# Three-part products with the low factors last, and transposes moved behind every second half-unit

## The chip, the cores and the metric

One core of a Trainium2 chip. The metric is the time of one execution on the device in microseconds; a kernel is run three times and the median is taken. One execution more is recorded by the hardware profiler. Its engines are called PE (TensorE), DVE (VectorE), ACT (ScalarE), POOL (GpSimd) and SP (SyncE) here, as in the profile.

## The reference

One inference step of a two-layer encoder for 512 frames of a new stream and 8 × 16 frames of running streams, 640 rows of 1024 values in all, float32. Each layer is a half-step SwiGLU FFN, a mixer, and another half-step FFN; each sub-layer ends in a layer norm:

```python
x = layer_norm(ALPHA * x + 0.5 * swiglu(x, ffn_w_gate[l, 0], ffn_w_up[l, 0], ffn_w_down[l, 0]), ...)
m = mixer_ab(...) if l % 2 == 0 else mixer_ssd(...)
x = layer_norm(ALPHA * x + m, ...)
x = layer_norm(ALPHA * x + 0.5 * swiglu(x, ffn_w_gate[l, 1], ffn_w_up[l, 1], ffn_w_down[l, 1]), ...)
```

The FFN is 1024 to 2816 to 1024. The first mixer is an S5 state-space model beside stick-breaking attention; the second is a Mamba-2 mixer (`mixer_ssd`): one projection to z, x, B, C and dt, a causal convolution of width 4, a chunked recurrence, a gate with an RMS norm, and an output projection. Nearly all of the arithmetic lies in the projections.

## The kernel before

**Three-part products.** Every float32 operand of a projection is held as two tiles of type float32r: a high part, made by a copy on ACT, and a low part, the rest, made by a subtraction on DVE (`split`, L99 to L101; one layer norm further, L210 and L211 do the same for x). A product of two such operands is three matmuls: high × high, low × high, high × low. They are added up in one PSUM bank over all K tiles of 128 rows. Three functions write such products:

- `mm3` (L140): the projections of both mixers, the first units and the down-projections of the FFNs. For each K tile it issues the three parts, then goes on to the next K tile.
- `product` in `ffn` (L362): the gate and up projections of all four FFNs multiply pairs of units by a seven-product scheme. Each of the seven is 4 K tiles × 3 parts with 320 columns.
- `product` in `down7` (L497): the same scheme for most of the down-projection in FFN 1 to 3, 2 K tiles × 3 parts with 512 columns.

The attention part of the first mixer has a list of matmuls of its own (`three`, issued at L1044 in an order that is fixed by hand).

**Stages.** They run in the order FFN 0, mixer 0, FFN 1, FFN 2, mixer 1, FFN 3. Activations `xt` are held channel by channel, once as high and once as low part, 8 K tiles of 640 columns. Channel-wise projections (`cm_proj`) handle them in two halves, `HALVES`: rows 0 to 255 (a matmul of 256 columns) and rows 256 to 639 (384 columns). One half of one unit of 128 output channels is called a half-unit here: 24 matmuls. Row-wise projections (`tm_proj`) add into `yacc`, 5 tiles of 128 rows, called t = 0 to 4.

**Layer norms and transposes.** `layer_norm` (L174) works on one tile t of `yacc`: statistics on DVE (L181, L182), the power on POOL (L184), and then for t < 4 a pass on ACT (L188), DVE (L190) and three on POOL (L191 to L193), for t = 4 two passes on DVE (L195, L197). After that the tile has to be turned for the next stage: eight transposes on PE (L209), whose results ACT (L210, high) and DVE (L211, low) copy out. They are not issued at once but put on a list, `pend`; `run_pend` (L165) issues the oldest entry. A stage ends with `run_pend` at t = 2, 3 and 4, so two entries, t = 3 and t = 4, are left for the stage behind it. There they are issued between the first half-units, which need only t = 0 and 1. Half-units of the second half need t = 2 to 4.

**The start of mixer 1.** `xbc_half(g, u, h)` computes half h of one unit of x, B or C, `gate_half` one of z, `dt_half` one of dt. Today each of the three ends in a `run_pend`. The first calls are

```python
xbc_half(0, 0, 0)
xbc_half(0, 1, 0)
dt_half(0)
gate_half(0, 0, 0)
xbc(0, 0)
```

where `xbc(0, 0)` starts with the second half of unit 0. Later calls find the list empty.

**What sets the order.** The program is written in the order of the source, and the framework gives each engine its instruction list: by priority in source order, with room to put an instruction behind another one whose operands it expects sooner. On the chip each engine then works its list off in order. Weights come by DMA from SP into 4 raw tiles, are converted by ACT and DVE, and wait in 6 pairs of tiles. Matmuls write 8 PSUM banks: kinds a (2), b (4), y and z (1 each).

## Time and profile before

| | |
|---|---|
| three runs | 2533.86, 2541.68, 2542.25 us; median 2541.68 |
| profiled execution | 2534.06 us; span from first to last instruction 2532.4 us |
| DVE busy | 2018.3 us (80% of the span) |
| ACT busy, POOL busy | 1272.1 us (50%), 372.9 us (15%) |
| granted clock of TensorE, mean | 0.997 |
| moved by DMA | 324.80 MB, 128 GB/s |

How to read it: a row of the timeline is "start, duration, engine, line, operation, output <- inputs, shape, count", with the idle time of the engine before it and what ended that in brackets. PE shows matmuls, PEld the loads of their stationary operand. Matmuls are pipelined: a row's duration is the time that one is under way, and the pace is read from start to start. "w" is a converted weight, "xhi" and "xlo" are the parts of x, "h" the FFN's hidden rows, "T" sums of blocks of x, "og" and "csb" the gated rows of mixer 1, "bank" a PSUM bank.

### The profile page before, as it was taken

The page shows a single profiled execution, that of the slowest core. Times are in us where ns is not written, and L with a number is a line of the kernel's source. Part 1 is how long each engine was busy: PE and PEld are TensorE (multiplying, and loading weights), DVE is VectorE, ACT ScalarE, POOL GpSimd, SP SyncE. Part 2 cuts the span into 40 slices and gives each one's busy share as a digit, 9 for nine tenths or more (in the row PEclk, how much of TensorE's full clock was granted, in tenths as well). Part 3 has the DMA queues.
Part 4 walks back from the last instruction along what each step waited for, and adds up shares of the span by engine and source line. Part 5 has one row for each costly group of instructions (what it writes and reads, how often), then busy time and mean ns, then how long its engine had stood idle before and what let it go on. Part 6 is the DMA issues. An engine that isn't in the chain of part 4 may idle for free. (4 is left out here: it accounts for less than half of the span.)

```text
span 2532.4 us, 40815 instructions
## 1 busy us (share of the span) xinstructions
PE 2488.3 (98%) x15551; PEld 2282.8 (90%) x15551; DVE 2018.3 (80%) x3505; ACT 1272.1 (50%) x2389; POOL 372.9 (15%) x492
## 2 busy tenths in 40 slices
PE   9999999999999999999999999999999999999998
PEld 8999999878779999999999999999999879999997
DVE  7788777666878888878988887777576789998887
ACT  4443444336744555553455554566565543554542
POOL 0000001210130000013000002311121151112121
PEclk9999999999999999999999999999999999999999
DMA  5332335443221433462144434456464722555563
GB/s 186 109 101 87 107 118 155 144 160 109 84 84 59 116 104 98 113 162 68 59 113 112 121 100 131 150 163 196 151 214 135 244 72 94 158 149 164 154 173 115
DMA packets 179253, 324.80 MB, mean 128 GB/s; under 512 B 21312, under 2 KB 92608, under 8 KB 178544
## 3 DMA queue, kind: packets, MB, share of 16 engines
q1 hardware_dynamic: 165200, 293.83, 36.7%
q0 software_dynamic: 13856, 28.35, 5.7%
q8 instruction: 122, 2.00, 0.3%
q14 instruction: 75, 0.61, 0.1%
HBM read 259.56 MB, written 40.54 MB: 119 GB/s over the span
## 5 line engine op out<-in xcount | busy, mean ns | idle before, releaser
L101 DVE TENSOR_TENSOR w<-raw,w 128x512 fp32r<-128x512 f32 (+2 forms) x721 | 626.4, 890 | 84.0 <-ACT w L100 81.2
L100 ACT CAST w<-raw 128x512 fp32r<-128x512 f32 (+1 forms) x721 | 531.5, 769 | 317.2 <-DVE raw L349 153.2
L366 PE MATMUL bank<-xhi,w 128*128 128x320 f32 x2432 | 540.4, 310 | 2.9 <-DVE s L408 1.9
L146 PE MATMUL bank<-xhi,w 128*128 128x256 f32 (+2 forms) x2272 | 497.6, 311 | 6.7 <-DVE hf L288 1.7
L366 PE MATMUL bank<-T,w 128*128 128x320 f32 x2736 | 428.4, 309 | 3.6 <-ACT bank L383 1.7
L366 PEld LDWEIGHTS bank<-xhi,w 128*128 128x128 f32 x2432 | 406.8, 188 | 8.7 <-DVE s L408 3.1
L366 PEld LDWEIGHTS bank<-T,w 128*128 128x128 f32 x2736 | 407.0, 188 | 6.6 <-ACT bank L383 3.9
L146 PEld LDWEIGHTS bank<-xhi,w 128*128 128x128 f32 x2272 | 376.9, 187 | 16.3 <-issue 3.9
L366 PE MATMUL bank<-xlo,w 128*128 128x320 f32 x1216 | 375.2, 309 | 0.0
L146 PE MATMUL bank<-xlo,w 128*128 128x256 f32 (+2 forms) x1136 | 350.5, 309 | 2.0 <-DVE xlo L211 1.8
L146 PE MATMUL bank<-w,h 128*128 128x512 f32 x1488 | 346.5, 391 | 0.0
L146 PEld LDWEIGHTS bank<-w,h 128*128 128x128 f32 x1488 | 277.1, 188 | 57.5 <-ACT h L100 1.4
L366 PEld LDWEIGHTS bank<-xlo,w 128*128 128x128 f32 x1216 | 228.2, 188 | 0.0
L146 PEld LDWEIGHTS bank<-xlo,w 128*128 128x128 f32 x1136 | 213.6, 188 | 3.3 <-DVE xlo L211 2.1
L349 DVE TENSOR_TENSOR raw<-raw 128x512 f32<-128x512 f32 x304 | 211.5, 696 | 3.4
L515 POOL DMA_DIRECT2D yacc<-ev x84 | 72.6, 888 | 689.4 <-ACT ev L514 610.8
L502 PE MATMUL bank<-w,h 128*128 128x512 f32 x576 | 134.5, 389 | 0.0
L502 PEld LDWEIGHTS bank<-w,h 128*128 128x128 f32 x576 | 108.1, 188 | 22.4
L379 ACT COPY mx<-bank 128x320 f32<-128x320 f32 x152 | 64.6, 425 | 104.4 <-PE bank L366 104.1
L511 DVE SCALAR_TENSOR_TENSOR yacc<-bank,yacc 128x512 f32<-128x512 f32 x84 | 57.8, 688 | 72.0 <-PE bank L502 71.9
L223 DVE SCALAR_TENSOR_TENSOR yacc<-bank,yacc 128x512 f32<-128x512 f32 x120 | 81.8, 686 | 34.1 <-PE bank L146 33.4
L514 ACT ACTIVATE ev<-bank 128x512 f32<-128x512 f32 x84 | 50.2, 597 | 116.2 <-PE bank L502 112.9
(437 smaller groups left out, 3427.6 us busy)
## 6 DMA issues: line engine op xcount, KB each, us to landing
raw<-in_w_gate_dram SPq DMA_DIRECT2D x88, 512.0 KB, 3.6
raw<-in_w_up_dram SPq DMA_DIRECT2D x88, 512.0 KB, 4.1
raw<-in_w_down_dram SPq DMA_DIRECT2D x88, 512.0 KB, 3.6
raw<-in_m_in_dram SPq DMA_DIRECT2D x52, 512.0 KB, 4.4
yacc<-ev POOLq DMA_DIRECT2D x84, 256.0 KB, 4.7
raw<-in_m_out_dram SPq DMA_DIRECT2D x24, 512.0 KB, 4.5
csb<-cs_d SPq DMA_DIRECT2D x20, 512.0 KB, 5.3
h<-in_ssd_h_dram SPq DMA_DIRECT2D x16, 512.0 KB, 6.1
```

The costliest lines, as they stand in the source:

```text
L100: nc.scalar.copy(hi, src)
L101: return nc.vector.tensor_tensor(lo, src, hi.bitcast(F32), op=ALU.subtract)
L146: state["pe"] = nc.tensor.matmul(ps, a, b, start=(k == 0), stop=(k == n - 1)).ins
L223: state["acc"] = nc.vector.scalar_tensor_tensor(ya, pb, scale, ya, op0=ALU.mult, op1=ALU.add).ins
L349: V.tensor_tensor(o, v, w, op=ALU.subtract)
L366: nc.tensor.matmul(ps, A[p][:, a, k * 128:k * 128 + 128], X[p][b][:, k, :], start=(first and n == 0), stop=(n == 11), skip_group_check=True)
L379: nc.scalar.copy(e[n], ps)
L502: nc.tensor.matmul(ps, a[:, u], b[:, v], start=(first and n == 0), stop=(n == 5), skip_group_check=True)
L511: V.scalar_tensor_tensor(ya, ps, 0.5 / ALPHA, ya, op0=ALU.mult, op1=ALU.add)
L514: nc.scalar.mul(e, ps, 0.5 / ALPHA)
L515: nc.gpsimd.dma_start(yacc[:, t, 512 * j:512 * j + 512], e, accum_op=ALU.add)
```

## The change

In the three functions the loop over parts becomes the outer one: high × high over all K tiles, then the two products with a low factor, each over all K tiles. In `product` of `ffn` the part with the low moving operand comes second and that with the low weights last; in the other two it is the other way about. The same matmuls add into the same banks. In mixer 1 the three helpers lose their `run_pend`, and two calls are put between the first half-units.

```diff
     def mm3(ps, lhs, rhs):
         n = 3 * len(lhs)
         k = 0
-        for (wh, wl), (xh, xl) in zip(lhs, rhs):
-            for a, b in ((wh, xh), (wl, xh), (wh, xl)):
+        for i, j in ((0, 0), (1, 0), (0, 1)):
+            for a, b in [(w[i], x[j]) for w, x in zip(lhs, rhs)]:
...
             def product(ps, A, p, first):
                 n = 0
-                for k in range(4):
-                    for a, b in ((0, 0), (1, 0), (0, 1)):
+                for a, b in ((0, 0), (0, 1), (1, 0)):
+                    for k in range(4):
                         nc.tensor.matmul(ps, A[p][:, a, k * 128:k * 128 + 128], X[p][b][:, k, :],
...
                 def product(ps, tp, p, first):
                     n = 0
-                    for f in fs[::2]:
-                        a, b = left(f, p, tp), right(f, p)
-                        for u, v in ((0, 0), (1, 0), (0, 1)):
+                    for u, v in ((0, 0), (1, 0), (0, 1)):
+                        for f in fs[::2]:
+                            a, b = left(f, p, tp), right(f, p)
...
                     nc.scalar.copy(es_[:, :, 3:19], ps[:, 512 - o:L].rearrange("p (b i) -> p b i", i=16))
-                run_pend()
...
                 V.scalar_tensor_tensor(s, s, 1.0, ps[:, :L], op0=ALU.add, op1=ALU.mult)
-                run_pend()
...
                 V.tensor_scalar(dt[:, o:o + L], ps[:32, :L], hp[:, 0:1], None, op0=ALU.add)
-                run_pend()
...
             xbc_half(0, 0, 0)
             xbc_half(0, 1, 0)
+            run_pend()
             dt_half(0)
             gate_half(0, 0, 0)
+            run_pend()
             xbc(0, 0)
```

## The prediction

> **What bounds the kernel now.** I read the page first: its span, its busy shares, then the waits of TensorE (columns: engine and line that waited, who ended the wait; us in total, times, longest).

> ```profile
> span 2532.4 us, 40815 instructions
> PE 2488.3 (98%) x15551; PEld 2282.8 (90%) x15551; DVE 2018.3 (80%) x3505; ACT 1272.1 (50%) x2389; POOL 372.9 (15%) x492
> ```

> ```profile
> PE bank L209 <- POOL yacc L192: 4.1, 2, 2.1
> ...
> PE bank L146 <- DVE xlo L211: 1.8, 1, 1.8
> ...
> PE bank L146 <- ACT xhi L210: 1.0, 4, 0.2
> ...
> PE bank L146 <- DVE og L101: 0.8, 1, 0.8
> PE bank L366 <- DVE w L101: 0.7, 1, 0.7
> ```

> TensorE has work in flight for 2488.3 of 2532.4 us, so all waits together are worth 44.1 us (1.7%), and the change adds and removes no instruction. It can act in two ways only: by the pace of the matmuls, or by the few waits that a low part or a pending transpose ends. Those are the five rows above. "bank" is the output; the releaser is what the matmul lacked: 4.1 us for a normalized row (half of it at the point the change moves), 1.8 for the low part of x, 0.8 and 0.7 for low parts of og and w.

> **Pace.** The groups of the lines view by shape (count, busy us, mean ns of one), and two places of the timeline (start, duration):

> ```profile
> L366 PE MATMUL bank<-xhi,w 128*128 128x320 f32 x2432 | 540.4, 310 | 2.9 <-DVE s L408 1.9 <-ACT mx L379 0.7 <-DVE hf L418 0.4
> L366 PE MATMUL bank<-T,w 128*128 128x320 f32 x2736 | 428.4, 309 | 3.6 <-ACT bank L383 1.7 <-ACT w L100 1.2 <-DVE w L101 0.7
> L366 PE MATMUL bank<-xlo,w 128*128 128x320 f32 x1216 | 375.2, 309 | 0.0
> ```

> ```profile
> 101.47 0.31 PE L366 MATMUL bank<-xlo,w 128*128 128x320 f32 x1
> 101.61 0.45 PE L366 MATMUL bank<-xhi,w 128*128 128x320 f32 x2
> 101.91 0.31 PE L366 MATMUL bank<-xlo,w 128*128 128x320 f32 x1
> ```

> From one xlo matmul to the next it takes 0.44 us for three, 147 ns each, and they start evenly (101.47, 101.61): the pair that shares its moving operand gains nothing over the pair that changes both. High and low operands take 310 and 309 ns. So the new order costs 0 in pace. Its bounds on both sides: the rows differ by 1 ns of one matmul, and some 13,000 matmuls come from the three edited functions, so ±13 us if that 1 ns were an effect of order. I take 0, since the difference has the size of the rounding.

> **Part 1, the second mixer's start.** Today transposes follow the first and the second half-unit. The change runs them after the second and the fourth.

> ```profile
> 1589.40 0.48 PE L146 MATMUL bank<-xhi,w 128*128 128x256 f32 x2
> ...
> 1592.10 0.28 PE L146 MATMUL bank<-xlo,w 128*128 128x256 f32 x1
> 1592.67 1.73 POOL L192 TENSOR_TENSOR yacc<-yacc,T 128x512 f32<-128x512 f32 x1
> ...
> 1594.45 1.09 PE L209 MATMUL bank<-ident,yacc 128*128 128x128 f32 x8 [2.08 <-POOL yacc L192]
> ...
> 1598.59 1.27 DVE L197 SCALAR_TENSOR_TENSOR yacc<-yacc,rs,T 128x1024 f32<-128x1024 f32 x1
> ...
> 1600.01 1.07 PE L209 MATMUL bank<-ident,yacc 128*128 128x128 f32 x8
> ...
> 1601.07 0.62 DVE L101 TENSOR_TENSOR w<-raw,w 128x512 fp32r<-128x512 f32 x1
> ...
> 1602.83 1.27 DVE L101 TENSOR_TENSOR w<-raw,w 128x512 fp32r<-128x512 f32 x2
> ...
> 1606.36 0.51 PE L146 MATMUL bank<-xhi,w 128*128 128x384 f32 x2
> ```

> ```profile
> 1595.30:1598.70 3.40, 3.40 (x19) 3.40 (x18) 3.40 (x8) 1.20 (x3) 1.75 (x3) 0.52 0.64 217
> ...
> 469.00:472.00 3.00, 2.55 (x15) 2.56 (x16) 0.99 (x2) 0.00 (x0) 0.00 (x0) 1.00 1.00 356
> ...
> 1700.00:1720.00 20.00, 20.00 (x145) 19.07 (x144) 14.58 (x26) 12.33 (x35) 2.96 (x8) 1.00 0.58 166
> ```

> The first half-unit runs from 1589.40 to 1592.2 (24 matmuls, 2.81 us). Then TensorE stands for 2.08 us, since GpSimd ends row t=3 only at 1594.40. In the windows view the next 3.40 us have a granted clock of 0.52 (the column behind POOL): another 3.40 × 0.48 = 1.6 us. So the stall costs 3.7 us. After the 1.81 us stall of the mixer 0 start (second row) the clock is 1.00.

> [...]

> After the change t=3 is due at 1589.40 + 2 × 2.81 = 1595.0, later than 1594.40: no stall. Eight transposes take 0.87 us (1600.01 less its tail), so the third and fourth half-unit end at 1601.5; t=4 (DVE L197, ended 1599.86) is ready by then, the transposes end at 1602.4. What is late next: the unit behind them reads t=4 at once, where today 5.5 us lie between; the four such places in the waits table cost 0.2 us each, and an activation stands ahead of the copies, so 0.5 us. The second-half unit then starts at 1602.9 against 1606.36: 3.5 us gained at most. Against it: the gate unit's weights. I take the conversion at 1601.07 for the second half of its low part and the pair at 1602.83 for the unit behind it. TensorE would reach those low weights after three half-units, eight transposes and 12 more matmuls, 1589.40 + 8.4 + 0.9 + 1.4 = 1600.1, and DVE has them at 1601.69: 1.6 us back, 1.9 gained. DVE runs without a break here (3.40 of 3.40 us in the first windows row), but its order will be dealt anew, and the transposes' low parts leave the way. I take 2.5 (range 1.9 to 3.5; 0.3 if the new stall reaches 2 us and halves the clock again). It stays gained: in the mixer behind it TensorE is the busy engine (last windows row: 20.00 of 20.00 us, DVE 14.58).

> **Part 2, low factors last.** The places where a low part ends a wait (and at the end of the list, DVE's busy time in 20 us around the last):

> ```profile
> 466.50 1.14 PE L146 MATMUL bank<-xhi,w 128*128 128x384 f32 x5 [0.24 <-ACT xhi L210]
> ...
> 468.71 1.28 DVE L211 TENSOR_TENSOR xlo<-bank,xhi 128x512 fp32r<-128x512 f32 x2
> ...
> 469.45 0.44 PE L146 MATMUL bank<-xlo,w 128*128 128x384 f32 x1 [1.81 <-DVE xlo L211]
> ...
> 2056.54 5.29 PE L146 MATMUL bank<-w,og 128*128 128x512 f32 x22 [0.77 <-DVE og L101]
> ...
> 2168.03 1.88 PE L366 MATMUL bank<-T,w 128*128 128x320 f32 x11 [0.73 <-DVE w L101]
> ```

> ```profile
> 2160.00:2180.00 20.00, 19.27 (x129) 18.68 (x129) 19.86 (x31) 12.23 (x23) 1.99 (x2) 1.00 0.38 122
> ```

> At mixer 0's start the second half-unit needs xlo after two matmuls. After the change 16 matmuls of 0.174 us go ahead (0.51 us for two less the 0.34 of one), so xlo is due at 466.50 + 2.8 = 469.3; DVE has the first half at 469.35, the second at 469.99, due at 470.0. Gain 1.8, at least 0 should the S5 part behind it wait for other engines instead. At 2056.54 the low part of og is needed after 4 matmuls instead of 1, 0.68 us later at 227 ns (5.29 us for 22, less the tail): 0 to 0.7, I take 0.5. At 2168.03 the low weights come 8 matmuls (1.2 us) later, which covers 0.73; but DVE is busy for 19.86 of 20 us there and only makes TensorE wait elsewhere: 0 to 0.7, I take 0.3.

> What could be lost: the high parts of the *last* k are needed sooner. At the start of the program:

> ```profile
> 8.18 0.39 PE L146 MATMUL bank<-xlo,w 128*128 128x256 f32 x1 [0.23 <-DVE xlo L101]
> ...
> 41.12 0.56 PE L146 MATMUL bank<-xhi,w 128*128 128x320 f32 x2 [1.74 <-DVE hf L288]
> ```

> The sweep over x is three times as fast as the loads and 18 low products are left behind the last load: up to 0.7 us later. TensorE waits for DVE at 41.12 for 1.74 us anyway, which hides it: 0 (without that cover 0.7). And at the end of each FFN:

> ```profile
> 422.89 16.81 PE L146 MATMUL bank<-w,h 128*128 128x512 f32 x72
> 423.33 0.48 DVE L416 TENSOR_TENSOR hf<-bank,s 128x320 f32<-128x320 f32 x1
> 423.45 1.35 ACT L100 CAST h<-hf 128x640 fp32r<-128x640 f32 x2 [0.97 <-DVE hf L420]
> ...
> 427.49 0.69 DVE L223 SCALAR_TENSOR_TENSOR yacc<-bank,yacc 128x512 f32<-128x512 f32 x1 [1.60 <-PE bank L146]
> ```

> The last down starts at 422.89, the last two rows of h get their high parts at 424.80, and there is no break in 72 matmuls. The first sum is read at 427.49, where one bank's 12 matmuls would end at 425.6: several banks are begun ahead of h. After the change each bank gives 2 matmuls that don't need the late rows; four banks give 8 × 227 ns = 1.8 us, to 424.7. That is 0.1 us short; four FFNs, 0.4 us lost.

> **Sum.** −2.5 − 1.8 − 0.8 + 0.4 = −4.7 us. The profiled execution took 2534.06 us (span 2532.4, 1.7 around it), so 2529.4 in its place. The three runs are 2533.86, 2541.68 and 2542.25: the profiled one lies by the lowest, the median is 7.6 above it. Against the median: 2541.68 − 4.7 = 2537.0. A measurement of this kernel tells about 0.5% (12.7 us) from no change, so this counts as the same.

> **Rivals.** *Absorbed.* The waits only move, since DVE (80% over all, 19.86 of 20 us in the stretch above) is late next: the gate's low weights, the S5 chain, the FFN. Then 0 to −1.5, 2541. For it: DVE is busy in every one of the 3.40 us behind the first stall. Against: TensorE is at 98%, and each wait of part 2 stands alone.

> *Less new than it says.* The order on the chip is not that of the source already: the row at 466.50 has five high products in a row where the loop gives two, so the low ones had been put off by whatever orders the program, and the rest of the gain is part 1 alone: −2.5, 2539. It also leaves out the hand-ordered products of mixer 0's attention, which have a list of their own.

> *Slower: high parts wanted too soon.* If at each FFN end only one bank is begun ahead, TensorE stands from 422.89 + 0.45 = 423.3 to 424.8, 1.5 us, four times 6, and the net is −4.7 − 0.4 + 6.0 = +0.9: 2542.6; should such a stall halve the clock as at 1594, 4 × 1.6 us more, 2549. It decides when fewer than four banks are free there. The row of 72 without a break speaks against it.

> *Pace.* ±13 us by the 1 ns: 2524 or 2550.

> **Chances.** Forecast 0.55, absorbed 0.17, less new 0.13, slower 0.10, pace 0.05 (half to each side). 2537.0 is the likeliest. Faster by over 0.5% means below 2529.0: a median as low as the lowest run would give 2529.4, so a quarter of the forecast's chance goes there, with the faster half of pace and a little of absorbed and less new (as low a median): 0.18. Slower by over 0.5% is above 2554.4: the clock case with more of such stalls, or pace: 0.04. Same 0.78. The range goes from the sum with the best ends of its terms (−3.5 − 1.8 − 1.4 = −6.7) from the profiled execution, 2534.06 − 6.7 = 2527.4, rounded down to 2526, to the slower case without the clock and some spread of the runs, 2545.

> **What would show it.** Right: no idle time before the transposes of mixer 1's first units, a clock of 1.00 in the 4 us behind, 2 to 3.5 us between first matmul and second-half unit gone; the row of xlo L211 gone from TensorE's waits; busy time of the three matmul lines unchanged, 147 ns from one 320-column matmul to the next. Wrong: a new wait for DVE w L101 of over 1.6 us before 1602, a wait for ACT h at the FFN ends, another mean for the same shape, or a change of over 6 us in a stage that the diff does not touch, which would mean that the whole order was dealt anew.

## The result and the profile after

| | before | changed |
|---|---|---|
| median of 6 runs each | 2540.56 us (2533.86 to 2542.25) | 2528.55 us (2524.01 to 2531.27) |
| ratio, 95% interval | | 0.9957, 0.9941 to 0.9972 |
| profiled execution | 2534.06 us, span 2532.4 | 2531.27 us, span 2529.6 |

The change made the kernel faster by 12.0 us between the medians, and by 0.43% in the ratio. The two profiled executions show only 2.8 us of that: the one of before lies at the fast end of its runs, the changed one is the slowest of its six. So one pair of profiles is not enough here, and the places below are averaged over several. The ratios leave out two executions of later variants that took 2849.61 us (E5) and 3173.78 us (E12), at mean clocks of 0.80 and 0.72.

The page and the waits of TensorE in the changed kernel:

```profile
span 2529.6 us, 40802 instructions
PE 2490.1 (98%) x15551; PEld 2286.1 (90%) x15551; DVE 2014.5 (80%) x3505; ACT 1269.2 (50%) x2389; POOL 373.5 (15%) x492
```

```profile
PE bank L1691 <- DMA bx<-bcx_d: 3.6, 3, 2.5
...
PE bank L146 <- ACT xhi L100: 2.6, 2, 2.4
...
PE bank L146 <- DVE yacc L1810: 1.4, 1, 1.4
...
PE bank L366 <- DVE w L101: 1.3, 1, 1.3
PE bank L146 <- ACT xhi L210: 1.2, 5, 0.2
```

The row for xlo L211 (1.8 us) is gone, and so are the 4.1 us for the norm's rows (POOL yacc L192), but for 0.4. New are waits for high parts at the start (xhi L100) and a longer wait for the load of bx. The low weights in the last FFN (w L101) are waited for 1.3 us where it was 0.7.

**Pace.** The lines view by shape, and the FFNs from 770 to 1575 us in one window, before and changed:

```profile
L366 PE MATMUL bank<-xhi,w 128*128 128x320 f32 x2432 | 436.2, 309 | 2.3 <-DVE s L408 1.4 <-ACT mx L379 0.7
L366 PE MATMUL bank<-T,w 128*128 128x320 f32 x2736 | 428.2, 310 | 5.3 <-ACT bank L383 2.7 <-ACT w L100 1.4 <-DVE w L101 1.3
...
L366 PE MATMUL bank<-xlo,w 128*128 128x320 f32 x1216 | 227.8, 309 | 0.0
```

```profile
770.00:1575.00 805.00, 804.76 (x4846) 757.56 (x4845) 668.27 (x1075) 409.71 (x690) 77.71 (x82) 1.00 0.39 106
```

```profile
770.00:1575.00 805.00, 804.76 (x4847) 757.37 (x4846) 668.23 (x1074) 409.33 (x691) 78.03 (x83) 1.00 0.39 105
```

The means are 309, 310 and 309 ns, as before. The column ahead of them fell a great deal (xlo from 375.2 to 227.8 us), and that says nothing on pace: it is the time in which any matmul of the group is under way, and high and low ones no longer alternate. In the window TensorE is busy for 804.76 of 805 us in both kernels.

**The two places that the prediction named.** The second mixer's start, by its timeline and in windows:

```profile
1592.98 1.09 PE L209 MATMUL bank<-ident,yacc 128*128 128x128 f32 x8
1599.37 1.03 PE L209 MATMUL bank<-ident,yacc 128*128 128x128 f32 x8
1600.64 1.66 PE L146 MATMUL bank<-xhi,w 128*128 128x384 f32 x8 [0.24 <-ACT xhi L210]
```

```profile
1590.00:1594.00 4.00, 4.00 (x37) 3.91 (x36) 4.00 (x9) 3.31 (x8) 3.17 (x3) 1.00 0.26 61
1594.00:1598.00 4.00, 4.00 (x37) 3.85 (x36) 3.92 (x7) 2.51 (x5) 4.00 (x8) 1.00 0.85 245
1598.00:1602.00 4.00, 3.76 (x30) 3.53 (x29) 4.00 (x11) 1.46 (x3) 0.39 (x3) 1.00 0.86 275
```

No idle time stands ahead of the transposes (L209), the clock (third column from the end) is 1.00, and the second-half unit starts at 1600.64 instead of 1606.36; 2.1 of these 5.7 us were gained before 1575 us already. At the first mixer's start 16 high products now run ahead of the first low one, without a gap:

```profile
468.98 3.10 PE L146 MATMUL bank<-xhi,w 128*128 128x384 f32 x16 [0.24 <-ACT xhi L210]
471.92 1.57 PE L146 MATMUL bank<-xlo,w 128*128 128x384 f32 x8
```

**Where the time went.** TensorE runs 15,551 matmuls in each kernel, so the starts of the matmuls with the same number can be subtracted. The table has the mean of seven profiled executions with the whole change (the changed kernel twice, and five variants of it from the experiments) less the mean of four with the old order (before twice, the transposes alone twice). A variant is left out where its own edit acts: at the start, from 1758 to 1780 us, and the transposes alone from 1575 to 1700 us. Times are those of the first profile of before.

| place (us) | gain or loss | foretold |
|---|---|---|
| 0 to 45, start | +0.4 (-1.0 to +2.4) | 0 |
| 45 to 466, first FFN | +0.2 | +0.1 |
| 466 to 475, first mixer's start | -3.5 | -1.8 |
| 475 to 770, rest of first mixer | -3.2 | none |
| 770 to 1575, two FFNs | 0.0 | +0.2 |
| 1575 to 1610, second mixer's start | -3.6 | -2.5 |
| 1610 to 1758 | -0.5 | none |
| 1758 to 1780, load of bx | +2.3 (+0.3 to +5.6) | none |
| 1780 to 2060 | +0.7 | -0.5 |
| 2060 to 2100, second mixer's last units | -3.9 | none |
| 2100 to the end, last FFN | +0.1 | -0.2 |
| sum | -11.0 | -4.7 |

The sum lies near the 12.0 us between the medians. Between 2025 and 2060 us the two orders issue their matmuls in a different sequence, so inside that stretch the same number is not always the same work; at 2060 it is again.

### The profile page after: what moved, and what is told of

The parts are those of the page before. It is cut to its first block, busy times and chain, and to the rows that moved or that the text cites. A ratio compares the mean times of both kernels' runs of the same rounds, so it can differ in the third digit from the quotient of the medians.

```text
span 2529.6 us, 40802 instructions
## 1 busy us (share of the span) xinstructions
PE 2490.1 (98%) x15551; PEld 2286.1 (90%) x15551; DVE 2014.5 (80%) x3505; ACT 1269.2 (50%) x2389; POOL 373.5 (15%) x492
## 5 line engine op out<-in xcount | busy, mean ns | idle before, releaser
L100 ACT CAST w<-raw 128x512 fp32r<-128x512 f32 (+1 forms) x721 | 532.7, 769 | 337.3 <-DVE raw L349 144.7
L101 DVE TENSOR_TENSOR w<-raw,w 128x512 fp32r<-128x512 f32 (+2 forms) x721 | 621.2, 883 | 86.9 <-ACT w L100 84.0
L366 PE MATMUL bank<-xhi,w 128*128 128x320 f32 x2432 | 436.2, 309 | 2.3 <-DVE s L408 1.4
L366 PE MATMUL bank<-T,w 128*128 128x320 f32 x2736 | 428.2, 310 | 5.3 <-ACT bank L383 2.7
L366 PEld LDWEIGHTS bank<-T,w 128*128 128x128 f32 x2736 | 406.8, 188 | 8.6 <-ACT bank L383 5.3
L366 PEld LDWEIGHTS bank<-xhi,w 128*128 128x128 f32 x2432 | 376.8, 188 | 6.6 <-DVE s L408 2.2
L146 PE MATMUL bank<-xhi,w 128*128 128x256 f32 (+2 forms) x2272 | 364.3, 312 | 5.2 <-ACT xhi L100 2.6
L146 PEld LDWEIGHTS bank<-xhi,w 128*128 128x128 f32 x2272 | 337.3, 189 | 15.8 <-issue 4.9
L146 PE MATMUL bank<-w,h 128*128 128x512 f32 x1488 | 346.5, 391 | 0.2 <-DVE yacc L223 0.2
L146 PEld LDWEIGHTS bank<-w,h 128*128 128x128 f32 x1488 | 277.2, 188 | 57.9 <-ACT h L100 1.6
L366 PE MATMUL bank<-xlo,w 128*128 128x320 f32 x1216 | 227.8, 309 | 0.0
L366 PEld LDWEIGHTS bank<-xlo,w 128*128 128x128 f32 x1216 | 190.8, 188 | 0.0
L146 PE MATMUL bank<-xlo,w 128*128 128x256 f32 (+2 forms) x1136 | 190.0, 309 | 0.0
L146 PEld LDWEIGHTS bank<-xlo,w 128*128 128x128 f32 x1136 | 171.6, 188 | 0.6
L379 ACT COPY mx<-bank 128x320 f32<-128x320 f32 x152 | 64.6, 425 | 105.9 <-PE bank L366 105.2
L223 DVE SCALAR_TENSOR_TENSOR yacc<-bank,yacc 128x512 f32<-128x512 f32 x120 | 82.0, 687 | 40.3 <-PE bank L146 39.7
L146 PE MATMUL bank<-w,og 128*128 128x512 f32 x432 | 103.1, 394 | 0.0
```

Of the source, the lines that this page charges most:

```text
L100: nc.scalar.copy(hi, src)
L101: return nc.vector.tensor_tensor(lo, src, hi.bitcast(F32), op=ALU.subtract)
L146: state["pe"] = nc.tensor.matmul(ps, a, b, start=(k == 0), stop=(k == n - 1)).ins
L223: state["acc"] = nc.vector.scalar_tensor_tensor(ya, pb, scale, ya, op0=ALU.mult, op1=ALU.add).ins
L366: nc.tensor.matmul(ps, A[p][:, a, k * 128:k * 128 + 128], X[p][b][:, k, :], start=(first and n == 0), stop=(n == 11), skip_group_check=True)
L379: nc.scalar.copy(e[n], ps)
```

## The experiments

Theories ahead of them. A: the gain is a sum of separate waits, each gone at its place. B: it is the moved transposes. C: it is the order of the products. All runs are compared with the kernel before on the same chip.

**The two halves of the change.** E1 has the moved transposes alone (one `run_pend` less in each of the three helpers, two calls between the units):

```diff
-                run_pend()
...
             xbc_half(0, 1, 0)
+            run_pend()
             dt_half(0)
             gate_half(0, 0, 0)
+            run_pend()
```

> The kernel before with the moved transposes alone (all products in their old order). Theory A, the gain is a sum of separate places: between the two profiled executions the second mixer's start gained 3.7 us (2.1 of idle and the half clock behind it), so 2540.6 - 3.7 = 2537 us, ratio 0.9985, and the other places (the first mixer's start, the second mixer's last units) stand as before. Rival B, the moved transposes are the whole gain of 12 us: 2528.5 us, ratio 0.9957. Rival C, the order of the products is the whole gain: 2540.6, ratio 1.000.

E2 has the order alone (the other half of the diff).

> The change without the moved transposes: high x high first in all three places, transposes where they were. Theory A: 2528.5 + 3.7 = 2532 us, ratio 0.9968; the wait for the low part of x at the first mixer's start is gone, the 2.08 us of idle at the second mixer's start is there and with it the clock at about half for 3.4 us. Rival B (moved transposes are all): 2540.6, ratio 1.000. Rival C (the order is all): 2528.5, ratio 0.9957.

E1: 2537.16 us, ratio 0.9993 (0.9985 to 1.0001). E2: 2530.3 us, 0.9962 (0.9951 to 0.9974). B is out; the order is most of the time. But A is not right either. At the second mixer's start (1575 to 1610 us) each half alone gains nothing, E1 +0.3 and E2 +0.1 us, where both together gain 3.6. The medians are too coarse to show this: by the ratios the halves gain 1.8 and 9.6 us and the whole 11.2 (E4 below), each with an interval of 2 us or more to either side. It rests on the places, where all seven profiles of the whole change gain 3.5 or 3.6 us and none of the others gains over 0.1. The timelines of E1 and of E2 there:

```profile
1597.48 1.04 PE L209 MATMUL bank<-ident,yacc 128*128 128x128 f32 x8
1603.97 1.04 PE L209 MATMUL bank<-ident,yacc 128*128 128x128 f32 x8
1607.68 1.97 PE L146 MATMUL bank<-xhi,w 128*128 128x384 f32 x5 [2.68 <-ACT xhi L210]
```

```profile
1589.89 1.97 PE L209 MATMUL bank<-ident,yacc 128*128 128x128 f32 x8 [2.55 <-POOL yacc L192]
```

In E1 the stall ahead of the transposes is gone and another of 2.68 us stands behind the last ones, with a clock of 0.50 from 1607.3 to 1610.7 us. In E2 the old stall is longer, 2.55 us, and the clock behind it is at half (0.50 from 1589.7 us on, for 3.4 us), as before.

**What E1's new wait is.** In E1 a weight load had come to stand ahead of the small load of hp on SyncE's queue and held it for 5.07 us; ScalarE waited for hp, and the copies of x stood behind that. E9 takes hp out of the way:

```diff
+            hp = const.tile([32, 2], F32, name="hp")
+            nc.sync.dma_start(hp, I["ssd_hd"])
             with after_norm():
...
-                hp = wk.tile([32, 2], F32, name="hp")
-                nc.sync.dma_start(hp, I["ssd_hd"])
```

> The moved transposes alone, with the 256-byte load of hp taken out of the group that waits for the norm (it gets a place that nobody else uses, and can be loaded at any time). In the run with the moved transposes alone the second mixer's start gained nothing (0.3 us later): a weight load had come to stand ahead of hp on SyncE's queue, held it for 5.07 us until 1601.28, ScalarE then waited until 1605.41 for hp, and the copies of the last transposes (0.57 us each) ended at 1608.1. Theory A (the new transposes' gain was lost to that queue order): the wait of 2.68 us ahead of the second half-unit goes down to 0.2 to 0.5, the place gains 2.5 to 3.6 us like in the change, ratio 0.9993 - 0.0011 = 0.9982, 2535 us. Rival: the copies are late for another reason (the splits of the weights on VectorE, the load of cw), the wait stays near 2.7 us and the ratio 0.9993.

E9: 2537.03 us, 0.9991 (0.9982 to 1.0000), and nothing gained at the place (-0.1 us). The queue made E1's wait, but clearing it gains nothing, so theory A falls. The timeline of E9 and the window behind:

```profile
1604.88 0.97 PE L146 MATMUL bank<-xhi,w 128*128 128x384 f32 x4 [0.24 <-ACT xhi L210]
1606.24 0.44 PE L146 MATMUL bank<-xhi,w 128*128 128x384 f32 x1 [0.39 <-DVE dt L1625]
1607.77 0.69 PE L146 MATMUL bank<-xlo,w 128*128 128x384 f32 x1 [1.09 <-DVE xlo L211]
```

```profile
1607.80:1611.20 3.40, 3.40 (x11) 3.40 (x12) 0.51 (x1) 0.00 (x0) 0.00 (x0) 0.54 0.99 366
```

The wait for the copies is down to 0.24 us, as theory A had it, and TensorE then stands after a few matmuls for VectorE, 1.09 us of it for the low part of x, with a clock of 0.54 for the next 3.4 us. That is the interaction: with the transposes moved, the next unit reads x at once, and in the old order it needs the low part after two products. The same place in the second run of the changed kernel (E4) shows 16 products that need the high part alone, and VectorE's row for the low part:

```profile
1597.06 1.04 PE L209 MATMUL bank<-ident,yacc 128*128 128x128 f32 x8
1598.34 3.04 PE L146 MATMUL bank<-xhi,w 128*128 128x384 f32 x16 [0.24 <-ACT xhi L210]
...
1599.97 1.27 DVE L211 TENSOR_TENSOR xlo<-bank,xhi 128x512 fp32r<-128x512 f32 x2
```

VectorE is no sooner here: it starts on the low part 2.9 us after the transposes begin (1597.06), in E9 3.4 us after. The first low product is due at 1601.22, when both rows of the low part are all but done, so nothing waits. The load of hp is in time in the changed kernel (issued at 1590.8 us in E4, at 1602.6 in E1); why its place in the queue differs is not shown.

**Which products.** E5 has the new order in `mm3` alone, E10 in `mm3` as the second mixer's output products call it, and nowhere else; in both the transposes stay.

> The kernel before with the new order in the general three-part product alone (projections, first and last units); the seven-product units and the down products keep their old order, the transposes stand where they stood. Theory A: all of the order's gain comes from waits at the mixers' edges, which this product feeds, and none from the seven-product units (the matmul indices between 770 and 1575 us keep their distance to within 0.1 us in every pair of profiles): ratio 0.9962 like the order alone, 2530 us. Rival: the seven-product units' order gives part of it at the FFNs' ends (2.3 us at the ends of the first FFN and at the last one): ratio 0.9970 to 0.9980.

```diff
+    def mm3(ps, lhs, rhs, high_first=False):
...
-                        [w_j(w, j) for w in wo[g]])
+                        [w_j(w, j) for w in wo[g]], high_first=True)
```

> The kernel before with the new order in the second mixer's output products alone. Theory A: the 3.55 us that every run with the new order gains between 2060 and 2082 us come from these products, the wait of 2.07 us for the last norm step of the first block goes and the spell at a clock of 0.60 behind it, and the 1.0 to 2.4 us lost between 1900 and 2040 come with it, so net -1.5 to -2.9 us, ratio 0.9990. Rival: they come from the order that the products of the projections leave on VectorE's queue before, and this kernel shows the 2.07 us wait as before; ratio 1.000.

E5: 0.9962 (0.9948 to 0.9975), the same as E2. The orders in the seven-product units and the down products give nothing that these runs can show; the rival's 0.9970 to 0.9980 lies for the most part outside the interval. E10: 2533.95 us, 0.9984 (0.9975 to 0.9992), somewhat more of a gain than A's 0.9990, which its interval includes. Its profiled execution is the slowest of its twelve (2539.11 us). In it -3.5 us between 2060 and 2082 as with the whole order, and 3.05 us lost between 1900 and 2040. The waits of TensorE from 2062 to 2100 us, before and in E10:

```profile
PE bank L209 <- POOL yacc L192: 2.1, 1, 2.1
PE bank L146 <- DVE yacc L1813: 1.7, 1, 1.7
```

```profile
PE bank L151 <- DVE yacc L1818: 1.4, 1, 1.4
```

So the second mixer's own output products take away the stall ahead of its first transposes. How, by VectorE's timeline of before and of E4 (the last sum of the first block's rows, then its norm's step L183):

```profile
2061.87 0.75 DVE L1813 SCALAR_TENSOR_TENSOR yacc<-bank,rms,yacc 128x512 f32<-128x512 f32 x1 [0.95 <-PE bank L146]
...
2065.12 0.14 DVE L183 TENSOR_SCALAR rs<-mv 128x1 f32<-128x1 f32 x1
```

```profile
2054.25 0.75 DVE L1810 SCALAR_TENSOR_TENSOR yacc<-bank,rms,yacc 128x512 f32<-128x512 f32 x1
...
2056.53 0.15 DVE L183 TENSOR_SCALAR rs<-mv 128x1 f32<-128x1 f32 x1
```

Before, two sums of other blocks stood in between on VectorE and the norm went on 2.5 us behind the sum, now 1.5 us; and now 37 matmuls (36 in the first profile of the change) instead of 29 lie between that sum and the transposes. Both come from the written-out order of the engines, dealt anew. That much is read from the traces; why the order came out so was not tried. The half clock behind the old stall is not what the place gains: E11, a second profile of before (below), has the stall of 2.09 us without it (clock 1.00 from 2060 to 2095 us), and then waits 3.06 us for VectorE (yacc L1813) near 2094 us where the first waited 1.68, so that the stretch from 2060 to 2100 us is equally long in both. VectorE sets its end, and the change brings VectorE's work forward.

**The start.** The first profile of the changed kernel lost 2.4 us there, to a wait for the later K tiles of x. E3 leaves the first four products K tile by K tile:

```diff
+        if state.get("by_k"):
+            pairs = [(w[i], x[j]) for w, x in zip(lhs, rhs) for i, j in order]
...
+                state["by_k"] = ph == "ffn0" and h == 0
```

> The change, with the first four products of the kernel (first half-units of units 0 and 1 of the first FFN) left K tile by K tile. Theory A: the changed kernel is 2.4 us behind at the end of the start (it waits 2.43 us for the high part of x's later K tiles, and its clock is at 0.50 from 10 to 15 us), and nothing later takes that up, so 2528.5 - 2.4 = 2526 us, ratio to before 0.9948. Rival: the lost 2.4 us come from the load of x that landed 1.4 us later in that one execution (8.19 against 6.78 us), not from the order, and this is 2528.5 like the change, ratio 0.9957.

E4 is the change once more.

> The change itself once more, as the measure for the others of this chip. Theory A: ratio 0.9957 within 0.9941 to 0.9972, and in its profile the same places as in the first one, but the spells of half clock may lie elsewhere: the wait for the DMA of bx at 1760 us (2.5 us, half clock for 8 us behind it) may be shorter or without the half clock, and the span is then 2522 to 2526 us. Rival: the wait at 1760 and its half clock belong to the change and are there each time, so its span is again near 2529 us.

E3: 2524.11 us, 0.9942 (0.9929 to 0.9954). E4: 2527.6 us, 0.9956 (0.9943 to 0.9969). E3's median is as A wanted, but its profile doesn't show the cause: at 45 us it stands 0.05 us ahead of before, E4 0.09 behind, E2 0.4 ahead, all three alike. Over the profiles the start comes out between -1.0 and +2.4 us with the new order, and between -0.5 and +0.9 with the old. In the first profile x had landed 1.4 us later than in that of before (8.19 against 6.78 us), so its loss says little of the order. What E3's better median comes from stays open. For the rest of E4, A was right: no half clock behind the wait for bx, and a span of 2522.5 us.

**The wait for bx.** A spell of half clock, here and in the expectations, is a stretch with a granted clock of 0.50. The first row of each pair is the wait, the second the window behind it, in the first profile of the changed kernel and in E4:

```profile
1759.58 0.77 PE L1691 MATMUL bank<-bx 128*128 128x128 f32 x2 [2.50 <-DMA bx<-bcx_d]
```

```profile
1764.00:1769.00 5.00, 5.00 (x23) 1.95 (x23) 1.16 (x2) 1.34 (x6) 0.00 (x0) 0.50 0.55 153
```

```profile
1757.47 0.46 PE L1691 MATMUL bank<-bx 128*128 128x128 f32 x2 [2.04 <-DMA bx<-bcx_d]
```

```profile
1764.00:1769.00 5.00, 5.00 (x35) 4.99 (x35) 2.34 (x7) 1.75 (x5) 0.08 (x1) 1.00 0.93 347
```

The wait differs by 0.5 us, the place by 5.3 (+5.6 against +0.3): in one the clock is at 0.50 for 10 us, in the other it stays at 1.00. What differs is where the wait falls. In the first profile of the changed kernel the clock changes at 670.65, 674.06, 1759.50 and 1769.74 us: 1, 318 and 3 times 3.413 us apart (more traces in the last section). In E4 it falls at 667.82 us, and 319 times 3.413 us behind that is 1756.68. Cut into stretches of that length at these points, the wait looks so in the first profile of the changed kernel and in E4 (the first busy time is that of TensorE):

```profile
1756.09:1759.50 3.41, 0.99 (x6) 0.67 (x4) 2.60 (x4) 1.66 (x4) 0.00 (x0) 1.00 0.95 288
1759.50:1762.91 3.41, 3.33 (x16) 3.36 (x16) 3.17 (x6) 3.41 (x14) 0.51 (x4) 0.50 0.80 261
```

```profile
1753.27:1756.68 3.41, 2.15 (x13) 1.83 (x11) 3.37 (x5) 2.10 (x4) 0.00 (x0) 1.00 0.93 288
1756.68:1760.09 3.41, 2.62 (x23) 2.63 (x23) 2.49 (x5) 2.97 (x8) 1.17 (x3) 1.00 0.81 287
```

In the one the whole wait lies in a single window, which is idle for 71%, and the next is at a clock of 0.50. In the other it is shared by two, idle for 37 and 23%, and neither is followed by a spell.

The 12 runs of the changed kernel fall into two groups, 5 from 2524.0 to 2526.2 and 7 from 2528.2 to 2531.3. E6 fills the idle time; E7 shortens the wait, with the stores in `core_s`, behind the next block's `core_a`:

```diff
+                if (g, c) == (1, 0):
+                    for _ in range(12):
+                        nc.tensor.matmul(pcb[:, 0:128], ident, ident, start=True, stop=True)
```

> The change, with 12 matmuls of the identity by itself (128 x 128, 0.109 us each, 1.3 us) put into the bank ahead of the first matmul on bx at one place, 1757 us, where the changed kernel waits 2.0 to 2.7 us for the load of bx. The wait for bx stays, the time in which nothing runs falls to 0.7 to 1.4 us. Theory A: the spell at a clock of 0.50 behind this wait, which cost 5.6 us in two of four profiles and nothing in the others, follows from the idle time; it is gone in every run, the upper group of runs (2528 to 2531 us) goes, and the median is 2525 us, ratio 0.9944. Rival: the spell comes from something else (the load on the 16 DMA engines, 0.98 busy there); runs fall into both groups as before, ratio 0.9957, and a profile can show the half clock though the matmuls ran.

```diff
-                    nc.sync.dma_start(xb_d[g][:, :, 0:512].rearrange("a t c -> t a c"), xs_.bitcast(F32))
-                    nc.sync.dma_start(xb_d[g][:, :, 512:640].rearrange("a t c -> t a c"), bs_.bitcast(F32))
+                    xbs[g] = xs_, bs_
...
+                xs_, bs_ = xbs.pop(g)
+                nc.sync.dma_start(xb_d[g][:, :, 0:512].rearrange("a t c -> t a c"), xs_.bitcast(F32))
+                nc.sync.dma_start(xb_d[g][:, :, 512:640].rearrange("a t c -> t a c"), bs_.bitcast(F32))
```

> The change, with the two stores of xb (640 KB) issued behind the load of bx for the next block and not ahead of it. Theory A: the load of bx is issued 1.0 us sooner (two issues of 0.45 us) and has 640 KB less ahead of it (1.8 us at 350 GB/s), so the wait of 2.0 to 2.7 us at 1757 us falls under 1 us and no half clock follows: 2527.6 - 2 us without a spell, and no run in the group at 2528 to 2531: median 2523 to 2525, ratio 0.9940. Rival: bx itself takes its 5.5 to 5.9 us beside the loads of the states (512 KB each), whatever stands ahead of it; 2527.6, ratio 0.9956.

E6: 2525.63 us (2523.43 to 2526.10), 0.9948 (0.9935 to 0.9960). E7: 2525.49 us (2523.93 to 2525.61), 0.9947 (0.9934 to 0.9959). None of these ten runs lies in the upper group, so A is right on the spells. On the waits it is not: in each another wait came up, as the timelines of E6 and of E7 show.

```profile
1764.13 0.65 PE L1778 MATMUL bank<-ident,xe 128*128 128x128 f32 x4 [1.61 <-DVE xe L1775]
```

```profile
1756.45 0.46 PE L1692 MATMUL bank<-bx 128*128 128x128 f32 x2 [0.44 <-DMA bx<-bcx_d]
1763.06 1.90 PE L1772 MATMUL bank<-h,ctm 128*32 128x512 f32 x4 [1.61 <-DMA h<-in_ssd_h_dram]
```

In E6 TensorE waits for xe instead. Its trace has 24 matmuls more, two for each of the 12, so the fillers took 24 × 0.109 = 2.6 us and not the 1.3 of the expectation, and covered the whole wait. In E7 the state h is late instead: its last load is now issued behind the two stores, at 1757.6 us, in E4 at 1754.4. Neither idle time, 1.61 us, was followed by half clock: the windows from 1755 to 1770 us are at 1.00 in both. E8 and E12 join E3's edit to E7's and to half of E6's:

> Both: the first four products K tile by K tile, and the stores of xb behind the load of bx. Theory A: 2524.1 of the first alone, less the spells at 1757 us that two of its six runs seem to have (2528) and less the 2 us of the wait: 2521 to 2522 us, ratio 0.9931. Rival: the two don't add, ratio 0.9942.

> The change, with the first four products K tile by K tile and six matmuls of the identity (12 passes of 0.109 us, 1.3 us) in the wait for bx at 1757 us. Theory A: no spell of half clock there; 2523 to 2524 us with no run above 2526.5, ratio 0.9938 to 0.9942, no better than the change with fillers alone (0.9948) by more than the intervals tell, since in the profiles the start came out at -1.0 to +2.4 us with the new order and at -0.1 to +0.9 us with the old one. Rival: the old order at the start is worth 2.4 us, as the first profile of the change said: ratio 0.9938 or below and a start 2 us sooner.

E8: 0.9942 (0.9929 to 0.9956). E12: 0.9944 (0.9931 to 0.9957). E8 came out as its rival has it, that the two don't add; A's 0.9931 lies at the edge of the interval. E12's profile has no spell and a start of -0.5 us, which speaks for its A. E3, E6, E7, E8 and E12 all beat the kernel before, with intervals that overlap each other's and the change's.

**A second profile of before.**

> The kernel before once more, for a second profile of it, since the profiled one (2534.1 us) was the second lowest of its runs and the median is 2540. Theory A: the runs of before near 2540 us hold one or two more spells of half clock (4 us of time each) behind idle stretches of over 2 us that the profiled one came through, above all the wait of 3.0 us at 669 us or that at 1765 us; the other places stand within 0.5 us. Rival: the difference of 6 us lies in the start or is spread over the whole span.

E11: 2539.33 us, profiled at 2539.03. It is 4.9 us behind the first profile: 1.9 us at the first mixer's start, 1.1 around 672 us, 1.2 between 1780 and 2060 us, 0.5 up to 466 us, 0.1 in the rest. Its first mixer's start:

```profile
470.39 0.69 PE L146 MATMUL bank<-xlo,w 128*128 128x384 f32 x1 [2.25 <-DVE xlo L211]
```

```profile
470.00:474.00 4.00, 3.61 (x12) 3.61 (x13) 0.93 (x2) 0.00 (x0) 0.00 (x0) 0.57 1.01 356
```

Theory A is right for the largest part, a spell of half clock that the first profile came through without; the others are a longer spell at 672 us (0.50 for 6.8 us, 3.4 in the first profile) and short waits. At 1598 us it waits 2.05 us without a spell (clock 1.00 from there to 1608 us), where the first profile had one.

## Why the prediction was right, and where its size was wrong

The likeliest class, within 0.5%, holds for the ratio (0.43%; its interval reaches 0.59%), and 2528.55 lies in the range. The sum was under half of the gain. That 2528.55 lies in the range is partly luck: the range's low end was the best ends of all terms, -6.7 us, taken from the fast profiled execution; taken from the median of before (2541.68) it would have been 2535, above the result.

- **Pace 0: right.** 804.76 us busy in both windows. The sign "busy time of the three lines unchanged" was ill chosen.
- **Part 1, -2.5: 3.6 measured, and the step was wrong.** The deduction of 1.6 us for the gate's low weights did not come, in E1 neither, where the products keep their old order: no row of its waits there names w. Worse, the 2.5 was given to the transposes alone. "The unit behind them reads t=4 at once ... so 0.5 us" priced the high part's copies and forgot the low part. In E1 the copies themselves were late, behind hp (2.68 us), in E9 the low part was; with the half clock behind it, either wait costs the whole gain. Both parts of the change were costed one by one, and the one hides what the other brings.
- **First mixer's start, -1.8: the mechanism right, the size -3.5.** The row said 1.81 us and a clock of 1.00 behind it. That was this one execution: in the other three of the old order a spell at 0.50 follows, 3.4 us from 470.7 us in E1, 470.9 in E9 and 470.3 in E11.
- **og, -0.5: the wait is gone, but others took its place.** No profile with the new order in these products shows the 0.77 us for the low part of og any more (five wait 0.2 to 0.4 us for its high part). In its stead each waits 0.9 to 1.3 us for xd near 2036, E10 too, and the row from 1780 to 2060 stands at +0.7.
- **Second mixer's last units: not in the prediction.** The same products gain the 3.9 us from 2060 to 2100, where the stall of 2.07 us at 2071 is gone. The prediction had the row in hand (4.1 us, two times) and asked of one half only.
- **Rest of the first mixer: not in the prediction.** In it a wait of 1.5 us for VectorE at 752 us is gone (-1.7 between 750 and 754), and 0.7 or 0.8 are gained between 550 and 600, in each profile with the new order but E10's. So products of mm3 other than the second mixer's output products bring it; how is not shown.
- **w, -0.3: wrong.** The wait of 0.73 us stays: 0.4 to 1.3 us in the seven profiles of the whole change, 0.6 or 0.7 in the four of the old order. The prediction's own doubt, VectorE busy for 19.86 of 20 us there, fits that; it was not tried.
- **FFN ends, +0.4: about right** (+0.2 in the first, 0.0 in the next two), and no wait for h of an FFN came.
- **Start, 0: right on average**, though one profile would have said +2.4.
- **Rivals.** *Absorbed* falls: the waits did not just move, but for those for bx and xd, where 2.3 and 0.7 us of the gain are given back. *Less new than it says* falls: E1 gains 1.8 us (its interval reaches zero) and E2 9.6. *Slower* and *Pace* did not come.

The stall of 2.08 us that the prediction read at 1592 us lies, in that trace, within one window of the kind that the last section counts, 1592.05 to 1595.47 us. It leaves the window idle for 61%, and the clock is at 0.50 right behind it.

## What to carry to other kernels

Two edits around one operand are not two terms of a sum: write down for each what the next reader needs first, and price the pair. Where TensorE is 98% busy, look for idle stretches of about 2 us, or several that add up to it within 3.4 us. In this kernel 26 of 38 stretches of 1.7 to 3.1 us had a spell of half clock behind them, which cost 1.7 us or more, and 12 had none; at the first mixer's start one profile of before had it (a clock of 0.57 from 470 to 474 us) and the other had not (1.00). So take two or three profiles of either kernel before subtracting places.

## What the hardware showed

In the 14 profiled executions, behind their first 60 us, TensorE stood idle 38 times for 1.7 to 3.1 us. Behind 26 of these the granted clock fell to 0.50: 7 of 15 up to 2.1 us, 7 of 8 from 2.2 to 2.7, 12 of 14 at 3.0 us (a stall that every execution has near 668 us), and not at the one of 3.06. Of 79 stretches of 0.95 to 1.68 us it fell behind four, each of which had other waits within 2 us.

| TensorE idle in the window | windows | followed by half clock |
|---|---|---|
| 55% and more | 23 | 23 |
| 42 to 55% | 25 | 8 |
| under 42% | 9909 | 0 |

Several short waits count together here: the waits of 0.94 us for xd and 0.70 us for zz in E4 leave one window idle for 48%, with a spell behind it. One wait under 1.7 us alone fills less than half of 3.413 us. The one of 3.06 us in E11 is shared by two windows (41 and 49%), and no spell followed. Between 42 and 55% the share does not tell which: in the first profile of before the spell at 2073 us stands behind a window idle for 51%, and the window from 1762.72 to 1766.13 us, idle for 50%, has none behind it. The ends of matmuls are modelled in the profile, so these shares are rough, and what sets the clock is not shown beyond these counts. Of the 31 spells 27 last 3.4 us (1.7 us lost), two last 6.8 (near 672 us in E10 and E11), and two, behind the load of bx in the first profile of the change and in E2, 10.2 us; in these last, TensorE was busy for 98% or more of each window, so idle time does not explain why they go on.
